# A hybrid decoder step on one core: operands of the second group made from x times g on ScalarE, without 1 / rms, and sums of weight blocks on VectorE

## The chip, the cores and the metric

The kernel runs on one core of a Trainium2 chip. A core has five engines with an instruction queue each, worked off in order: TensorE (PE: matmuls; PEld: its weight loads), VectorE (DVE), ScalarE (ACT), GpSimd (POOL) and SyncE (SP, which here issues the DMAs). Matmul results land in PSUM banks, everything else lies in SBUF. The metric is the device time of one execution in microseconds, as a median of runs.

## The reference, cut to what matters

One decoder layer for 1024 prompt tokens and 64 decode tokens, D = 1024, all in float32. After three mixers (a recurrence, a short convolution and an attention) whose outputs are `mixed`, it ends in

```python
x = x + mixed @ lw['w_out']
h2 = rmsnorm(x, lw['g_mlp'])
x = x + jnp.square(jax.nn.relu(h2 @ lw['w_up'])) @ lw['w_down']
gate = jax.nn.sigmoid(rmsnorm(x, lw['g_ple']) @ lw['w_ple_gate'])
x = x + gate * (p @ lw['w_ple_proj'])
# rmsnorm(x, g) = x * rsqrt(mean(x * x) + 1e-6) * g;  w_up is 1024 x 4096, w_down 4096 x 1024
```

1 / rms is one number for each token. It can be multiplied in ahead of the product with `w_up`, or after it and ahead of the square, since relu(r * a) = r * relu(a) for r > 0.

## The kernel before, in words

x is kept transposed: 8 blocks of 128 rows (features) by tokens. A float32 product is made from pieces: each operand is split into a high and a low part (`S.copy` to the high part on ScalarE, a subtraction for the low part on VectorE or GpSimd), and three matmuls are summed.

The tokens are cut in two groups, A (512) and B (576, "the second group"). Their MLPs run over 16 slices `fb` of 256 columns of w_up. For A, `up` (L1333) does 2 x 24 matmuls of 128x512, `down` (L1400) 8 x 6. A's 1 / rms is multiplied in after the matmuls, when the bank is read (L1341). For B, `up7` (L1348) makes each slice with 7 products of 12 matmuls of 128x288 in place of 8, from sums and differences of blocks of the weights and of x. The operands of the 7 products (x times gain times 1 / rms, in sums and differences, split in high and low) are made once, by `operands` (L1291), in two calls: ids 11, 2, 3, 4 into four buffers (tag "big" of pool `mpb`) that held B's mixed operands `mh`, `ml` until then, and ids 21, 1, 22 into pool `hpb`, which takes the room of A's operands `nh`, `nl`. Per k = 0 to 3 a call makes `hk` (features k and 4 + k; L1302), `tk` (differences; L1308 to L1314) and each operand's high part (L1316, ScalarE) and low part (L1317). `hk` and `tk` share four buffers, so that two k are in flight.

Per slice `up7` loads two raw pieces of w_up (tile `wr`, two buffers, 512 KB each), splits three blocks (`wh`, `wl`), makes four sums of blocks (`s0` to `s3`, L1354 to L1358, GpSimd before) and splits these (`wsh`, `wsl`, L1042 ScalarE and L1043 GpSimd). A piece's buffer is free for the next load when its casts, its subtractions and its sums are done. Products go to banks 0 to 3 in turn and are put together by VectorE (L1385: `c`, `u`, `v`), then relu and square (L1379), `ah` (L1380, ScalarE) and `al` (L1381, GpSimd). B's `down` writes banks 4 to 7 in turn and VectorE adds each to x (L1406); it is emitted a slice behind `up7`.

The order is the program's, moved by a scheduler at build time; each engine then works its own queue in order. Around the change it is: out_proj(B) (L1322: x of B += mixed @ w_out, two blocks of x for each slice of weights), last `up` of A, the last two `down` of A with B's `rms` and `operands` among them, then 16 rounds of `up7` and `down` of B, then the gate stage.

Of the kernel before, what the change touches and what calls it, by code (L numbers as in the profile page):

```python
# [24 lines left out]
AF = mybir.ActivationFunctionType  # L25
ALU = mybir.AluOpType
# [22 lines left out]
def hybrid_step(ctx: ExitStack, tc: tile.TileContext, I, O):  # L49
# [6 lines left out]
    def f(t):  # L56
        return t.bitcast(F32)
# [19 lines left out]
    acc = banks(0, 1, 2)  # L77
# [59 lines left out]
    def P1(name, i=0):  # L137
        return par[:, col[name] + i:col[name] + i + 1]
# [1065 lines left out]
    class Part:  # L1204
# [85 lines left out]
        def operands(self, gain, ids, pool, bufs):  # L1290


            n = self.n // 2
            out = {}
            for i in ids:
                t = pool.tile([128, 4, 2 * n], F32R, name=f"op{i}", tag="big", bufs=bufs)
                out[i] = t.rearrange("p k t -> p (k t)").rearrange("p (e k t) -> p e k t", e=2, k=4)
            need = set(ids)
            for k in range(4):
                h = self.act("hk", F32)  # L1300
                for e in range(2):
                    V.scalar_tensor_tensor(h[:, e], self.x[:, 4 * e + k], P1(gain, 4 * e + k), self.rb, op0=ALU.mult,  # L1302
                                           op1=ALU.mult)
                t = self.act("tk", F32)
                val = {11: h[:, 0, :n], 21: h[:, 1, :n], 22: h[:, 1, n:], 1: t[:, 0, :n], 2: t[:, 0, n:],
                       3: t[:, 1, :n], 4: t[:, 1, n:]}
                if need & {1, 2, 4}:
                    V.tensor_sub(val[1], h[:, 0, n:], val[11])  # L1308
                if need & {2, 4}:
                    V.tensor_sub(val[2], val[22], val[1])  # L1310
                if 4 in need:
                    V.tensor_sub(val[4], val[21], val[2])
                if 3 in need:
                    V.tensor_sub(val[3], val[22], h[:, 0, n:])  # L1314
                for i in ids:
                    S.copy(out[i][:, 0, k], val[i])  # L1316
                    (V if i in (21, 1, 22) else G).tensor_sub(out[i][:, 1, k], val[i], f(out[i][:, 0, k]))  # L1317
            return out

    w_up, w_down = I["w_up"][0], I["w_down"][0]  # L1320

    def out_proj(p, k0=0, nk=8, bank=acc):  # L1322
        nm = 16 // nk
        x = [h[k0 // 4:] for h in p.h]
        for m0 in range(0, 8, nm):
            w = load(w_out[k0 * 128:(k0 + nk) * 128, m0 * 128:(m0 + nm) * 128], nk, nm * 128)
            for m in range(m0, m0 + nm):
                for t0, n in p.chunks:
                    ps = bank()
                    gemm_p(ps, w, m - m0, x, t0, n, nk=nk)  # L1330
                    V.tensor_add(p.x[:, m, t0:t0 + n], ps[:, :n], p.x[:, m, t0:t0 + n])  # L1331
# [15 lines left out]
    def up7(p, fb, ops, pool):  # L1347
# [3 lines left out]
        a = {(m, k): r[k][:, :, 128 * m:128 * m + 128] for m in range(2) for k in range(2)}  # L1351
        s_ = [pool.tile([128, 512], F32, name=f"s{i}").rearrange("p (k c) -> p k c", k=4) for i in range(4)]
        w = {11: split_piece(a[0, 0])}
        G.tensor_add(s_[0], a[1, 0], a[1, 1])  # L1354
        G.tensor_sub(s_[1], s_[0], a[0, 0])
        G.tensor_sub(s_[2], a[0, 0], a[1, 0])
        w[12] = split_piece(a[0, 1])
        G.tensor_sub(s_[3], a[0, 1], s_[1])  # L1358
        w[22] = split_piece(a[1, 1])
        for i in (2, 1, 3, 4):  # L1360
            w[i] = split_piece(s_[i - 1], pool=pool, tag="ws", bufs=4)
# [14 lines left out]
        def out(m, e, c):  # L1376

            t = slice(e * n, e * n + n)
            V.scalar_tensor_tensor(c, c, 0.0, c, op0=ALU.max, op1=ALU.mult)  # L1379
            S.copy(ah[:, m, t], c)  # L1380
            G.tensor_sub(al[:, m, t], c, f(ah[:, m, t]))  # L1381

# [49 lines left out]
    for fb in range(1, NA):  # L1432
        u, before = up(A, fb), u
        down(*before)
    out_proj(B)
    B.rms(banks(6, 7))
    ops = B.operands("g_mlp", (11, 2, 3, 4), mpb, 4)
    for fb in range(NA, 16):
        u, before = up(A, fb), u
        if fb < 15:  # L1440
# [101 lines left out]
```

## Time and profile before

| | us |
|---|---|
| median of 3 runs (lowest, highest) | 1780.79 (1775.39, 1781.9) |
| profiled execution, its own time | 1778.32 |
| its span in the trace | 1776.6 |
| PE / DVE / ACT / POOL busy in the span | 1687.8 / 1097.3 / 743.7 / 746.1 |

How to read the rows below. A row of busy times names a stretch, its length, the busy us of each engine with the number of its instructions in brackets, the granted TensorE clock (1.00 is full), the busy share of the DMA engines and GB/s. A row of waits says which engine and line waited for which, with the total in us, how often and the longest. A row of a group names line, engine, operation, tile written <- tiles read, shapes, count, then busy us, mean ns of one, and the idle time ahead of them with its releaser. A row of a source answer gives durations as min/median/max in ns. A row of a timeline gives start and duration in us. Matmuls are pipelined: a busy PE is not a PE at full rate, and the pitch from start to start tells the rate. Buffer numbers are left out of names: `op` is any operand, `b` any bank, `s` any sum.

### The profile page before, as it was taken

Reading aid. Unit: us, or ns where it says so; the run is one execution under the profiler, and the core shown is the slowest. Engines: PE = TensorE matmul, PEld = TensorE weight load, DVE = VectorE, ACT = ScalarE, POOL = GpSimd, SP = SyncE. Lnnn points to the kernel's source line nnn. Section 1 sums busy time; section 2 is a strip of 40 time slices with the busy share of each in tenths; the row PEclk is TensorE's granted clock in tenths of the full one; section 3 lists DMA queues with packets and bytes.
Section 4 is the critical chain, followed back from the end, with each engine's and each line's share of the span. In section 5 each row is a group of like instructions: output and inputs, shape, how many; then the busy total and the mean of one; then the engine's idle time right before and its main releaser. Section 6 shows DMA issues by size and latency. Waiting matters only on the chain.

```text
span 1776.6 us, 30204 instructions
## 1 busy us (share of the span) xinstructions
PE 1687.8 (95%) x11741; PEld 1504.5 (85%) x11741; DVE 1097.3 (62%) x1788; ACT 743.7 (42%) x1459; POOL 746.1 (42%) x694
## 2 busy tenths in 40 slices
PE   6999899999999899999989999996989999999998
PEld 5898888888988778888866667985989999998898
DVE  6266954554676689887743434349867777677432
ACT  6634223323453567656533333433433333335421
POOL 4123322312301444323255532428887877764210
PEclk9999998999999899999999999998999999999999
DMA  5134356434524654433255544420333233232211
GB/s 182 50 118 134 107 150 174 117 90 118 138 81 132 190 165 123 123 122 93 85 149 167 168 132 130 134 72 24 95 95 96 88 92 96 84 93 63 74 51 39
DMA packets 206738, 196.98 MB, mean 111 GB/s; under 512 B 57794, under 2 KB 172130, under 8 KB 206467
## 3 DMA queue, kind: packets, MB, share of 16 engines
q1 hardware_dynamic: 201474, 178.27, 34.4%
q0 software_dynamic: 5120, 16.78, 3.2%
q8 instruction: 92, 1.51, 0.4%
q14 instruction: 52, 0.42, 0.1%
HBM read 158.02 MB, written 36.98 MB: 110 GB/s over the span
## 4 chain that ended last, share of the span: by engine, by line
PE 72%; DVE 12%; DMA 5%; issue 4%; ACT 3%; POOL 2%; SPq 2%; ACTq 0%; DVEq 0%; POOLq 0%
PE b L1062 12%; PE b L1064 12%; PE b L1063 12%; PE b L1369 3%; PE b L169 3%; PE b L1371 3%; PE b L1370 3%; PE b L170 3%; PE b L171 2%; PE b L790 2%; PE b L791 1%; PE b L792 1%; PE b L910 1%; DVE x L1406 1%; PE b L1192 1%
## 5 line engine op out<-in xcount | busy, mean ns | idle before, releaser
L1043 POOL TENSOR_TENSOR wl<-wr,wh 128x512 fp32r<-128x512 f32 x164 | 226.9, 1389 | 239.4 <-ACT wh L1042 220.0
L1042 ACT CAST wh<-wr 128x512 fp32r<-128x512 f32 x292 | 179.0, 623 | 342.7 <-PE b L1063 200.0
L1062 PE MATMUL b<-ah,wh 128*128 128x288 f32 (+1 forms) x768 | 257.2, 335 | 15.0 <-DVE x L1406 13.4
L1406 DVE TENSOR_TENSOR x<-b,x 128x288 f32<-128x288 f32 (+1 forms) x384 | 195.8, 528 | 95.4 <-PE b L1064 94.2
L1064 PE MATMUL b<-ah,wl 128*128 128x288 f32 (+1 forms) x768 | 252.7, 329 | 0.0
L1063 PE MATMUL b<-al,wh 128*128 128x288 f32 (+1 forms) x768 | 252.3, 329 | 0.0
L1062 PEld LDWEIGHTS b<-ah,wh 128*128 128x128 f32 x768 | 144.9, 189 | 33.4 <-DVE x L1406 17.8
L1062 PE MATMUL b<-nh,wh 128*128 128x512 f32 (+1 forms) x448 | 166.3, 372 | 2.5 <-DVE x L1331 1.6
L1063 PE MATMUL b<-nl,wh 128*128 128x512 f32 (+1 forms) x448 | 165.9, 370 | 0.0
L1064 PE MATMUL b<-nh,wl 128*128 128x512 f32 (+1 forms) x448 | 164.8, 368 | 0.0
L1064 PEld LDWEIGHTS b<-ah,wl 128*128 128x128 f32 x768 | 144.9, 189 | 10.3
L1063 PEld LDWEIGHTS b<-al,wh 128*128 128x128 f32 x768 | 145.3, 189 | 9.4 <-issue 0.8
L1043 DVE TENSOR_TENSOR wl<-wr,wh 128x512 fp32r<-128x512 f32 x128 | 110.7, 869 | 50.2 <-ACT wh L1042 46.2
L790 PE MATMUL b<-wh,h_hi 128*128 128x256 f32 x432 | 128.7, 298 | 2.0 <-ACT nat L797 2.0
L792 PE MATMUL b<-wh,h_lo 128*128 128x256 f32 x432 | 126.7, 293 | 0.0
L791 PE MATMUL b<-wl,h_hi 128*128 128x256 f32 x432 | 126.7, 293 | 0.0
L169 PE MATMUL b<-h_hi,wh 128*128 128x384 f32 (+1 forms) x336 | 115.9, 345 | 1.9 <-ACT xs L330 1.2
L890 DVE TENSOR_TENSOR_SCAN keep<-keep,onesq 128x128 f32<-128x128 f32 (+3 forms) x64 | 93.3, 1463 | 33.7 <-ACT keep L889 33.2
L170 PE MATMUL b<-h_lo,wh 128*128 128x384 f32 (+1 forms) x336 | 113.7, 338 | 0.0
L171 PE MATMUL b<-h_hi,wl 128*128 128x384 f32 (+1 forms) x336 | 112.9, 336 | 0.0
L159 POOL TENSOR_TENSOR wl<-wr,wh 128x1024 fp32r<-128x1024 f32 x26 | 68.8, 2656 | 94.1 <-ACT wh L158 94.1
L1062 PEld LDWEIGHTS b<-nh,wh 128*128 128x128 f32 x448 | 84.7, 189 | 18.8 <-DVE x L1406 2.6
(416 smaller groups left out, 4381.8 us busy)
## 6 DMA issues: line engine op xcount, KB each, us to landing
wr<-in_w_up SPq DMA_DIRECT2D x64, 512.0 KB
wr<-in_w_down SPq DMA_DIRECT2D x64, 512.0 KB
wr<-in_w_in SPq DMA_DIRECT2D x26, 512.0 KB
wr<-in_w_out SPq DMA_DIRECT2D x16, 512.0 KB
xt<-in_x_prompt SPq DMA_DIRECT2D x8, 512.0 KB
stk_s<-sth SPq DMA_DIRECT2D x32, 128.0 KB
stk_s<-stl SPq DMA_DIRECT2D x32, 128.0 KB
out<-nat SPq DMA_DIRECT2D x16, 256.0 KB
```

Of the source, the lines that this page charges most:

```text
L169: PE.matmul(ps[:, :n], wh[:, k, c], a, start=(k == 0), stop=False)
L170: PE.matmul(ps[:, :n], wh[:, k, c], b, start=False, stop=False)
L171: PE.matmul(ps[:, :n], wl[:, k, c], a, start=False, stop=(k == nk - 1))
L790: PE.matmul(o, a, w[0][:, k, :], start=(k == 0), stop=False)
L791: PE.matmul(o, a, w[1][:, k, :], start=False, stop=False)
L792: PE.matmul(o, b, w[0][:, k, :], start=False, stop=(k == 7))
L1042: S.copy(h3, src)
L1043: (sub or G).tensor_sub(l3, src, f(h3))
L1062: PE.matmul(ps[:, :n], w(0, k, m), a, start=(k == 0), stop=False)
L1063: PE.matmul(ps[:, :n], w(0, k, m), b, start=False, stop=False)
L1064: PE.matmul(ps[:, :n], w(1, k, m), a, start=False, stop=(k == nk - 1))
L1406: V.tensor_add(p.x[:, m, t0:t0 + n], ps[:, :n], p.x[:, m, t0:t0 + n])
```

## The change

Four edits:

- `operands` makes `hk` with ScalarE's copy with a scale (x times gain), 1 / rms left out. `out` of `up7` multiplies it in instead: relu(c) * rb on VectorE (where relu(c) * c stood), then a square on ScalarE as an instruction more.
- The low parts of the operands alternate between VectorE and GpSimd in place of a fixed share (VectorE for 21, 1 and 22, GpSimd for the others).
- The four sums of weight blocks of each `up7` move from GpSimd to VectorE.
- out_proj(B) works through its slices of w_out in the order 0, 4, 2, 6, so that blocks 0, 1, 4, 5 of x are final halfway, and the first call of `operands` stands ahead of `rms`.

```diff
             for k in range(4):
                 h = self.act("hk", F32)
                 for e in range(2):
-                    V.scalar_tensor_tensor(h[:, e], self.x[:, 4 * e + k], P1(gain, 4 * e + k), self.rb, op0=ALU.mult,
-                                           op1=ALU.mult)
+                    S.activation(h[:, e], self.x[:, 4 * e + k], AF.Copy, scale=P1(gain, 4 * e + k))
...
-                for i in ids:
+                for a, i in enumerate(ids):
                     S.copy(out[i][:, 0, k], val[i])
-                    (V if i in (21, 1, 22) else G).tensor_sub(out[i][:, 1, k], val[i], f(out[i][:, 0, k]))
+                    (V, G)[(a + k) % 2].tensor_sub(out[i][:, 1, k], val[i], f(out[i][:, 0, k]))
...
-    def out_proj(p, k0=0, nk=8, bank=acc):
+    def out_proj(p, k0=0, nk=8, bank=acc, order=None):
...
-        for m0 in range(0, 8, nm):
+        for m0 in order or range(0, 8, nm):
...
-        G.tensor_add(s_[0], a[1, 0], a[1, 1])
-        G.tensor_sub(s_[1], s_[0], a[0, 0])
-        G.tensor_sub(s_[2], a[0, 0], a[1, 0])
+        V.tensor_add(s_[0], a[1, 0], a[1, 1])
+        V.tensor_sub(s_[1], s_[0], a[0, 0])
+        V.tensor_sub(s_[2], a[0, 0], a[1, 0])
         w[12] = split_piece(a[0, 1])
-        G.tensor_sub(s_[3], a[0, 1], s_[1])
+        V.tensor_sub(s_[3], a[0, 1], s_[1])
...
-            V.scalar_tensor_tensor(c, c, 0.0, c, op0=ALU.max, op1=ALU.mult)
+            V.scalar_tensor_tensor(c, c, 0.0, p.rb[:, t], op0=ALU.max, op1=ALU.mult)
+            S.square(c, c)
...
-    out_proj(B)
+    out_proj(B, order=(0, 4, 2, 6))
+    ops = B.operands("g_mlp", (11, 2, 3, 4), mpb, 4)
     B.rms(banks(6, 7))
-    ops = B.operands("g_mlp", (11, 2, 3, 4), mpb, 4)
```

Three places show how the queues change, all in VectorE's. The first is where A's last down ends and the first round of `up7` begins; `x<-b` with 128x512 is the addition that frees a bank of A's down, L1302 makes `hk`, L1308 makes `tk`, op_12624 is operand 21, op_12625 operand 1, op_12626 operand 22. Before:

```order
L1406 TENSOR_TENSOR x<-b_12603,x 128x512
L1302 SCALAR_TENSOR_TENSOR hk<-x,par,rb 128x576 x2
L1406 TENSOR_TENSOR x<-b_12611,x 128x512
L1317 TENSOR_TENSOR op_12624<-hk,op_12624 128x288
L1317 TENSOR_TENSOR op_12625<-tk,op_12625 128x288
L1317 TENSOR_TENSOR op_12626<-hk,op_12626 128x288
```

After (the low parts are L1316 there, the sums L1353 to L1357):

```order
L1406 TENSOR_TENSOR x<-b_12603,x 128x512
L1406 TENSOR_TENSOR x<-b_12611,x 128x512
L1353 TENSOR_TENSOR s_12675<-wr 128x512
L1355 TENSOR_TENSOR s_12677<-wr 128x512
L1316 TENSOR_TENSOR op_12624<-hk,op_12624 128x288
L1316 TENSOR_TENSOR op_12626<-hk,op_12626 128x288
L1354 TENSOR_TENSOR s_12676<-s_12675,wr 128x512
L1316 TENSOR_TENSOR op_12625<-tk,op_12625 128x288
L1307 TENSOR_TENSOR tk<-hk 128x288
L1357 TENSOR_TENSOR s_12678<-wr,s_12676 128x512
```

The sixteen `hk` are gone from between the additions, and the `tk` of the first call have moved ahead of A's downs. The four sums, which stood in GpSimd's queue before, now come right behind A's last addition, between the low parts of the second call.

The second is a round of B in the steady state (`x<-b` with 128x288 frees a bank of B's down). Before:

```order
L1406 TENSOR_TENSOR x<-b_14939,x 128x288
L1406 TENSOR_TENSOR x<-b_14947,x 128x288
L1406 TENSOR_TENSOR x<-b_14955,x 128x288
L1385 TENSOR_TENSOR c<-b_15052,p_15037 128x288
L1379 SCALAR_TENSOR_TENSOR c<-c 128x288
L1406 TENSOR_TENSOR x<-b_14963,x 128x288
```

After:

```order
L1406 TENSOR_TENSOR x<-b_14939,x 128x288
L1406 TENSOR_TENSOR x<-b_14947,x 128x288
L1353 TENSOR_TENSOR s_15344<-wr 128x512
L1406 TENSOR_TENSOR x<-b_14955,x 128x288
L1354 TENSOR_TENSOR s_15345<-s_15344,wr 128x512
L1357 TENSOR_TENSOR s_15347<-wr,s_15345 128x512
L1406 TENSOR_TENSOR x<-b_14963,x 128x288
```

Three of the four sums now stand among the additions that free down's banks; the first of them, s0, reads both raw pieces of w_up.

The third is later in a round, where the last products are put together. Before:

```order
L1385 TENSOR_TENSOR c<-b_15120,v 128x288
L1379 SCALAR_TENSOR_TENSOR c<-c 128x288
L1385 TENSOR_TENSOR c<-b_15138,u_15113 128x288
L1379 SCALAR_TENSOR_TENSOR c<-c 128x288
L1043 TENSOR_TENSOR wl<-wr,wh 128x512
L1406 TENSOR_TENSOR x<-b_15176,x 128x288
```

After:

```order
L1385 TENSOR_TENSOR c<-b_15154,v 128x288
L1355 TENSOR_TENSOR s_15659<-wr 128x512
L1378 SCALAR_TENSOR_TENSOR c<-c,rb 128x288
L1385 TENSOR_TENSOR c<-b_15173,u_15146 128x288
L1378 SCALAR_TENSOR_TENSOR c<-c,rb 128x288
L1043 TENSOR_TENSOR wl<-wr,wh 128x512
L1406 TENSOR_TENSOR x<-b_15212,x 128x288
```

The fourth sum, s2, comes in ahead of a relu, and so ahead of the next four additions.

## Rows read from the trace of the kernel before

**Rows 1.** Busy time of each engine in stretches of the span

```profile
1190.00:1260.00 70.00, 50.23 (x261) 42.44 (x260) 66.62 (x84) 24.39 (x55) 51.99 (x42) 0.90 0.12 35
1260.00:1350.00 90.00, 84.38 (x615) 83.06 (x614) 64.91 (x113) 32.80 (x64) 78.00 (x62) 0.98 0.33 98
1350.00:1575.00 225.00, 225.00 (x1693) 225.00 (x1692) 158.16 (x289) 77.18 (x148) 180.31 (x141) 1.00 0.30 90
```

**Rows 2.** Busy time in stretches of 10 us, for the granted clock

```profile
1230.00:1240.00 10.00, 4.84 (x23) 4.32 (x21) 10.00 (x9) 4.47 (x10) 8.38 (x6) 0.67 0.01 2
...
1320.00:1330.00 10.00, 9.56 (x59) 9.42 (x60) 6.43 (x15) 2.96 (x6) 6.48 (x6) 0.83 0.23 71
```

**Rows 3.** PE's matmuls by form, 1190 to 1260 (first of three alike)

```profile
L1062 PE MATMUL b<-ah,wh 128*128 128x512 f32 x31 | 12.8, 412 | 4.8 <-DVE x L1406 4.8
```

**Rows 4.** Timeline of PE in A's down: two starts, 17 matmuls apart

```profile
1193.16 0.40 PE L1062 MATMUL b<-ah,wh 128*128 128x512 f32 x1
...
1197.03 0.39 PE L1064 MATMUL b<-ah,wl 128*128 128x512 f32 x1
```

**Rows 5.** What PE waited for, 1150 to 1360

```profile
PE b L1370 <- DVE op L1317: 11.0, 4, 5.2
PE b L1062 <- DVE x L1406: 10.3, 7, 2.7
PE b L1369 <- DVE x L1406: 2.1, 1, 2.1
```

**Rows 6.** VectorE's instructions by form, 1190 to 1260

```profile
L1302 DVE SCALAR_TENSOR_TENSOR hk<-x,par,rb 128x576 f32<-128x576 f32 x16 | 17.7, 1142 | 0.2 <-ACT rb L1282 0.2
L1406 DVE TENSOR_TENSOR x<-b,x 128x512 f32<-128x512 f32 x16 | 10.8, 679 | 0.7 <-PE b L1064 0.7
L1317 DVE TENSOR_TENSOR op<-hk,op 128x288 fp32r<-128x288 f32 x8 | 8.1, 1043 | 0.0
L1308 DVE TENSOR_TENSOR tk<-hk 128x288 f32<-128x288 f32 x8 | 6.8, 852 | 0.0
```

**Rows 7.** VectorE's lines of products and weights: durations, the whole span

```profile
L1379 DVE SCALAR_TENSOR_TENSOR c<-c x64: 449/1066/1617, 1247.5 to 1606.0; 128x288 f32<-128x288 f32 x64
L1385 DVE TENSOR_TENSOR c<-b,u x32: 442/458/460, 1247.1 to 1605.5; 128x288 f32<-128x288 f32 x32
L1043 DVE TENSOR_TENSOR wl<-wr,wh x37: 674/691/1786, 1360.1 to 1574.9; 128x512 fp32r<-128x512 f32 x37
```

**Rows 8.** ScalarE's instructions by form, 1190 to 1260 and 1177 to 1190

```profile
L1316 ACT CAST op<-hk 128x288 fp32r<-128x288 f32 x12 | 4.9, 430 | 9.6 <-DVE hk L1302 9.6
L1042 ACT CAST wsh<-s 128x512 fp32r<-128x512 f32 x8 | 4.5, 614 | 0.0
...
L1260 ACT ACTIVATE sq<-x 128x576 f32<-128x576 f32 x1 | 0.7, 685 | 0.1
```

**Rows 9.** GpSimd's sums and subtractions by form, 1350 to 1575

```profile
L1043 POOL TENSOR_TENSOR wsl<-s,wsh 128x512 fp32r<-128x512 f32 x36 | 53.3, 1503 | 0.5
...
L1354 POOL TENSOR_TENSOR s<-wr 128x512 f32<-128x512 f32 x10 | 13.0, 1296 | 21.6 <-DMA wr<-in_w_up 21.6
```

**Rows 10.** What the DMA queue waited for before it issued, 1350 to 1575

```profile
SPq L1036 <- POOL s L1355: 72.7, 10, 8.1
```

**Rows 11.** Timelines of VectorE in a round of B, and of GpSimd and PE there

```profile
1421.84 0.46 DVE L1406 TENSOR_TENSOR x<-b,x 128x288 f32<-128x288 f32 x1 [0.34 <-PE b L1064]
...
1422.99 1.29 POOL L1354 TENSOR_TENSOR s<-wr 128x512 f32<-128x512 f32 x1 [1.92 <-DMA wr<-in_w_up]
...
1423.43 0.46 DVE L1406 TENSOR_TENSOR x<-b,x 128x288 f32<-128x288 f32 x1 [1.14 <-PE b L1064]
...
1435.67 1.48 DVE L1379 SCALAR_TENSOR_TENSOR c<-c 128x288 f32<-128x288 f32 x1
...
1441.36 1.54 DVE L1406 TENSOR_TENSOR x<-b,x 128x288 f32<-128x288 f32 x4
...
1442.40 0.30 PE L1062 MATMUL b<-ah,wh 128*128 128x288 f32 x1
```

## The prediction

> **What bounds the kernel now.** The page comes first: PE is busy for 95% of the span, so the question is where PE does not run at its pitch. The table of busy times by stage answers it. From 1350 to 1575 us, the steady rounds of B, PE has 1693 matmuls in 225.00 us and never waits: 0.1329 us each [rows 1], so that a round of 84 + 96 matmuls takes 23.9 us. That is the rate of a bound PE, and nothing that frees another engine can gain there. The two stretches ahead of it are not at that rate.
>
> 1190 to 1260 us is the hand-over from A to B. Of its 261 matmuls 94 have 512 columns (three lines of 31, 31 and 32 [rows 3]), at a pitch of (1197.03 - 1193.16) / 17 = 0.228 us [rows 4]; 157 have 288 columns; ten small ones take 1.0 us together (an estimate; the rows below do not hang on it). At full pitch that is 94 x 0.228 + 157 x 0.1329 + 1.0 = 43.3 us of 70. **26.7 us are lost.** 1260 to 1350 us has 615 matmuls, 81.7 us of work in 90: **8.3 us lost** [rows 1].
>
> Why, is in what PE waited for: low parts of operands from VectorE (11.0 us) and VectorE's additions that free banks (10.3 and 2.1 us) [rows 5]. VectorE was busy for 66.6 of the 70 us [rows 1]. Of that the `hk` took 17.7, the additions of A's down 10.8, low parts and `tk` most of the rest [rows 6]. What is not a wait is the clock: after the waits it was granted at 0.67 from 1230 to 1240 [rows 2], which is in the 26.7. So the hand-over is bound by VectorE's queue.
>
> **The change part by part.**
>
> *`hk` to ScalarE.* It takes 17.7 us out of VectorE's 66.6 and adds 16 ScalarE instructions of about 0.69 us (a square of the same 128x576 tile takes 685 ns [rows 8]): 11 us on an engine that was busy for 24.4 of the 70 us [rows 1]. Without 1 / rms, half of the first call's `hk` and `tk` move ahead of 1177 us, into out_proj(B). No more than half: `hk` and `tk` have four buffers, and the operands themselves are written into the buffers of `mh` and `ml`, which out_proj(B) reads to its end. The order 0, 4, 2, 6 is what makes these two k possible, and costs nothing by itself, as the loads and matmuls are the same in number.
>
> *What is late next in the hand-over.* A's last two downs run with nothing between VectorE's additions, 0.68 us each [rows 6] against six matmuls of 0.228 = 1.37 us in PE: the waits for additions end. ScalarE has to deliver the high part of A's last `up` before the last down; in its queue that stands behind casts, `hk` and six of the squares of `rms`, and I count it there only 1 to 2 us early. I take 2 us lost (0 to 8). Then PE has operand 11 (12 matmuls, 1.6 us) and two k of operand 21 (0.8 us) to run, 2.4 us. The next matmuls want the cast of s1, which ScalarE does behind the copy of the first product (1.6 us, then 0.4) and four `hk` (4 x 0.69): 1.6 + 0.4 + 2.8 + 0.61 [rows 8] = 5.4 us, so PE waits 3.0. VectorE has s1 earlier, since GpSimd's queue is empty there. Behind that come the last k of the low parts and the four splits of the sums on GpSimd (1.29 to 1.5 us each [rows 9]), and banks that wait for VectorE behind the next round's sums: 4 us by the same count. So 7 us (3 if only the first wait shows, 12 if VectorE's instructions take their contended time). For the clock after a wait I take 2 us (0 to 3): 1320 to 1330, at 0.83 after one wait, had 59 matmuls where 75 fit [rows 2], 2.1 us. The hand-over keeps 2 + 7 + 2 = 11 of 26.7 and **gives back 15.7** (3.7 to 23.7).
>
> *Sums to VectorE, 1260 to 1350.* Here GpSimd was busy for 78 of 90 us [rows 1], and a raw buffer was freed by its sums: in the rounds after, the DMA queue waited 72.7 us for s1 alone [rows 10]. Four sums of 1.30 us [rows 9] leave GpSimd in each round of about 24 us, and on VectorE one takes from 0.69 us (the same shape as `wl` [rows 7]). Weights of down land earlier; I leave 2 us (0 to 6), so **6.3 come back** (2.3 to 8.3).
>
> *Sums on VectorE, every round.* In the steady rounds nothing can be gained, and VectorE goes from 158.2 / 225 = 70% busy [rows 1] to 70% + 4 x 0.69 / 24 = 82% or, at the longest time in the row of `wl`, 1.79 us [rows 7], to 100%. Two places matter. s0 waits for the second raw piece, which in the round shown landed when GpSimd's s0 started, 1422.99; VectorE comes to it after its third addition of that quarter, about 1421.5. The fourth, which started at 1421.84, slips to about 1423.7 and the next one by 2 us [rows 11]; with four banks PE comes back to a bank three groups of 0.80 us after it left it, so this is just hidden. s2 lies tighter: four additions from 1441.36 on free the banks of down, at 0.385 us each, the first by 1441.75, and PE wants that bank at 1442.40 [rows 11]: 0.65 us to spare. s2 takes 0.69 us if alone (0.04 lost) and about 1.3 if it stands behind a GpSimd instruction (0.65 lost). GpSimd's own s2 has left that place, so part of the time comes back. I take 0.25 us a round, 14 rounds: **3.5 us** (0 to 9).
>
> *The factor moved behind the matmuls* costs VectorE nothing: relu(c) * rb has the shape of relu(c) * c. ScalarE gets 64 squares of 128x288, 0.43 us each going by the cast of that shape [rows 8], four a round: 1.7 us on an engine busy for 77.2 / 225 = 34%. The square lengthens the way from `c` to `al`, but down of that slice runs a round later. Free, unless that lag is lost; then 0.43 us a round, 6 us.
>
> *Low parts in turns* moves 2 us from one engine to the other and is inside the counts above.
>
> On contention the rows speak against moving sums to VectorE. Its relu, which reads SBUF alone, takes 449 ns at best and 1066 in the median, while the addition of a bank to an SBUF tile of the same shape takes 442 to 460 [rows 7]: something holds up what reads SBUF twice. The Trainium skill (SBUF — State Buffer, Who interferes with whom) states that a VectorE instruction with two SBUF inputs contends with a GpSimd instruction that reads SBUF, and that the one that comes second waits for the whole of the other. The trace agrees as far as these two rows go. By the rule alone each of four sums a round would wait out a GpSimd instruction.
>
> **The sum.** 15.7 + 6.3 - 3.5 = 18.5 us. Against the profiled execution's 1778.3 that is 1759.8; the median of the runs is 2.5 above that execution, so **1762**.
>
> **Rivals.**
>
> *ScalarE becomes the limit of the hand-over.* Its queue gets the 16 `hk` ahead of the high part of A's last `up`, and I count that part only 1 to 2 us early. For it: the queue is in order, and each wait for a buffer of `hk` pushes all that follows. Against: it is busy for a third of the time. If it is 8 us late in place of 2, and the products wait 10 in place of 7, 9 us of the gain go: 1771. Chance 0.17.
>
> *Contention takes more.* By the mechanism of the relu row, every s2 stands behind a GpSimd instruction: 0.65 x 14 = 9 us in place of 3.5, so 1767.5; this is what the rule on SBUF would do here. Chance 0.15.
>
> *VectorE bounds the rounds: slower.* If the second raw piece lands late against VectorE's queue, s0 holds additions and PE stands in all 14 rounds. The place is the quarter with 1421.84; the price is what s0's wait exceeds the hidden 2 us by. The hand-over and the stretch after it give 22.0, so from 1.6 us a round it decides; at 2.5 us a round it is 35 - 22 = 13 us slower: 1794. For it: the landing follows VectorE's own `wl`, so a late VectorE makes it later still. Against: s1 and s3 on VectorE free the raw buffers sooner, and the average load is 82%. Chance 0.10.
>
> *More comes back.* With contention gone on both sides the hand-over keeps only 5 us and the rounds cost nothing: 21.7 + 8.3 = 30, 1751. Chance 0.13.
>
> That the operands don't get ahead at all (the order of x's blocks useless, since their buffers are held) is not a rival with a sign of its own: `hk` still leaves VectorE's queue.
>
> **How the numbers follow.** The forecast (1762, by its own bounds 1754 to 1772) has 0.45. The range takes in the two dearer cases and the cheaper one and leaves out most of the slower one: 1750 to 1780. What a measurement of this kernel can tell from no change is about 0.5%, 9 us: faster is below 1772, slower above 1790. Faster: 0.45 x 0.95 + 0.17 x 0.5 + 0.15 x 0.8 + 0.13 = 0.76; slower 0.08, as the slower case begins at its deciding point; the same 0.16.
>
> **What would show it.** In the profile after, 1190 to 1260 should have VectorE well below 66 of 70 us and PE near 60 busy, with few waits of PE for operands and no clock under 0.8; the next 90 us should have over 650 matmuls. In the rounds PE's pitch should stay at 0.133; a pitch over 0.14 with PE waiting for VectorE's additions would show the slower case. I am wrong in the first step if PE in the hand-over waits for ScalarE's `ah` or for casts of sums by more than 10 us.

## The result, and the profile after

After: 1767.19 us (median of 6 runs, 1761.68 to 1769.77); before, on the same chip, 1781.35 (6 runs, 1775.39 to 1787.41). The ratio is **0.9916, 95% interval 0.9889 to 0.9942**: 15 us faster (10 to 20), where 1762 and 18.5 us had been forecast. The profiled execution took 1763.72 us (span 1762.0) against 1778.32.

Not all of that difference of 14.6 us is the change. I set marks on program points in the timelines of PE and ScalarE: the last matmul of out_proj(B); the copy of `p` (L1389), once per round of `up7`, the first and the sixth of them; and the last matmul of B's last down. The outer two in PE's timeline of the kernel after (columns as in [rows 11]):

```profile
1174.73 0.29 PE L1064 MATMUL b<-mh,wl 128*128 128x288 f32 x1
...
1633.71 0.29 PE L1064 MATMUL b<-ah,wl 128*128 128x288 f32 x1
```

That is 458.98 us; the kernel before has 1177.12 and 1648.34 there, 471.22. So **the change is worth 12.2 us** in this pair of profiles. What lies behind the last mark is 128.3 us in both, and 2.4 us lie ahead of the first. Executions scatter more than that there: a kernel below (e4), whose queues are those of the kernel after up to that point, reached it at 1170.55. So these 2.4 us can't be credited to the change.

The windows that answer [rows 1], with the one ahead of them (busy us of PE, PEld, DVE, ACT, POOL with their counts, granted clock, DMA share, GB/s):

```profile
1177.00:1190.00 13.00, 11.65 (x52) 9.32 (x50) 13.00 (x16) 11.22 (x24) 9.60 (x9) 1.00 0.23 63
1190.00:1260.00 70.00, 57.63 (x331) 51.18 (x332) 58.98 (x81) 36.94 (x77) 46.24 (x36) 0.95 0.21 64
1260.00:1350.00 90.00, 88.23 (x655) 87.07 (x655) 70.92 (x132) 36.03 (x71) 50.13 (x41) 1.00 0.32 98
1350.00:1575.00 225.00, 224.38 (x1679) 223.21 (x1678) 178.60 (x328) 94.96 (x189) 121.71 (x104) 1.00 0.29 86
```

VectorE fell from 66.6 to 59.0 us in the hand-over and GpSimd from 78 to 50 in the stretch behind it; VectorE rose from 158 to 179 in the steady rounds, GpSimd fell from 180 to 122. By the forecast's own count, 1190 to 1260 now has 84 matmuls of 512 columns, 227 of 288 and 20 small ones: 19.1 + 30.2 + 2.0 = 51.3 of 70, so **18.7 us are lost in place of 26.7**. The next 90 us lose 90 - 655 x 0.1329 = 3.0 in place of 8.3. New is a loss of 1.1 us ahead of 1190 (52 matmuls of 512 columns in 13 us), where VectorE is busy for all of the 13 us.

What PE waited for from 1170 to 1300, which answers [rows 5] (us in total, times, longest):

```profile
PE b L1062 <- DVE x L1406: 5.6, 9, 1.7
PE b L1368 <- DVE c L1385: 2.4, 1, 2.4
PE b L1062 <- DVE r L1340: 2.4, 1, 2.4
PE b L1368 <- DVE u L1385: 2.2, 1, 2.2
PE b L1368 <- ACT wsh L1042: 2.0, 1, 2.0
PE b L1369 <- DVE op L1316: 0.9, 2, 0.6
```

The 11.0 us for low parts have shrunk to 0.9. But the engine that is late is still VectorE, in five rows of six. One of its stops, in the second round of B (VectorE's timeline):

```profile
1247.85 0.69 DVE L1353 TENSOR_TENSOR s<-wr 128x512 f32<-128x512 f32 x1 [1.57 <-DMA wr<-in_w_up]
1248.58 1.82 DVE L1354 TENSOR_TENSOR s<-s,wr 128x512 f32<-128x512 f32 x1
1250.31 0.44 DVE L1385 TENSOR_TENSOR u<-b,u 128x288 f32<-128x288 f32 x1
1250.68 1.38 DVE L1357 TENSOR_TENSOR s<-wr,s 128x512 f32<-128x512 f32 x1
1251.99 0.44 DVE L1385 TENSOR_TENSOR c<-b,u 128x288 f32<-128x288 f32 x1
```

The sum s0 holds the queue for its load, s1 and s3 take 1.82 and 1.38 us beside GpSimd in place of 0.69, and the `c` for which PE waits 2.4 us stands behind them.

### The profile page after: what moved, and what is told of

Its sections match the earlier page's. It is cut to its first block, busy times and chain, and to the rows that moved or that the text cites. A ratio compares the mean times of both kernels' runs of the same rounds, so it can differ in the third digit from the quotient of the medians.

```text
span 1762.0 us, 30342 instructions
## 1 busy us (share of the span) xinstructions
PE 1683.0 (96%) x11741; PEld 1500.2 (85%) x11741; DVE 1115.4 (63%) x1838; ACT 779.8 (44%) x1539; POOL 649.7 (37%) x628
## 4 chain that ended last, share of the span: by engine, by line
PE 68%; DVE 14%; DMA 6%; issue 4%; ACT 3%; SPq 2%; POOL 2%; ACTq 0%; DVEq 0%; POOLq 0%
PE b L1062 12%; PE b L1064 11%; PE b L1063 11%; DMA wr<-in_w_up 3%; PE b L1368 2%; PE b L1370 2%; PE b L1369 2%; PE b L169 2%; PE b L170 2%; PE b L171 2%; DVE x L1406 2%; PE b L790 2%; DVE wl L1043 2%; PE b L791 1%; PE b L792 1%
## 5 line engine op out<-in xcount | busy, mean ns | idle before, releaser
L1406 DVE TENSOR_TENSOR x<-b,x 128x288 f32<-128x288 f32 (+1 forms) x384 | 191.7, 527 | 68.8 <-PE b L1064 66.2
```

## The experiments

All in one table: us from out_proj(B)'s last matmul to the first copy of p, from there to the sixth, from there to B's last down, the sum, and the ratio to the kernel before, with its 95% interval. In the rows with a star the scheduler gave PE another order of the rounds, and more of the work stands ahead of the sixth copy of p: 788 matmuls of 288 columns behind the first mark in e2, 774 in f1 and 789 in e4, where the kernel after has 749 and the one before 747. At 0.1329 us each their second part is too long, and their third too short, by 5.2, 3.3 and 5.3 us. The sum does not suffer.

| kernel | to p 1 | p 1 to p 6 | p 6 to down | sum | ratio (interval) |
|---|---|---|---|---|---|
| before | 45.5 | 124.3 | 301.4 | 471.2 | 1 |
| after | 42.3 | 115.6 | 301.1 | 459.0 | 0.9916 (0.9889, 0.9942) |
| e1: sums alone | 44.4 | 125.3 | 309.3 | 479.0 | 1.0046 (1.0025, 1.0067) |
| e2: all but the sums* | 42.7 | 121.4 | 306.1 | 470.2 | 0.9988 (0.9967, 1.0009) |
| g1: sums and square | 44.4 | 122.0 | 300.9 | 467.3 | 0.9977 (0.9959, 0.9996) |
| f1: e2, third raw buffer* | 42.6 | 118.9 | 296.3 | 457.8 | 0.9925 (0.9897, 0.9953) |
| f2: e1, third raw buffer | 46.3 | 124.1 | 318.6 | 489.1 | 1.0135 (1.0102, 1.0167) |
| f3: after, third raw buffer | 43.8 | 114.7 | 300.1 | 458.5 | 0.9944 (0.9923, 0.9965) |
| e4: sums of two rounds back* | 42.7 | 127.3 | 308.5 | 478.6 | 1.0006 (0.9985, 1.0027) |
| e3: old order of out_proj | 42.3 | 115.8 | 300.9 | 458.9 | 0.9919 (0.9887, 0.9950) |
| e5: low parts on VectorE | 42.8 | 117.1 | 303.1 | 462.9 | 0.9940 (0.9919, 0.9960) |
| e6: low parts on GpSimd | 39.0 | 116.5 | 301.2 | 456.6 | 0.9901 (0.9875, 0.9927) |
| g2: first p on VectorE | 43.8 | 117.1 | 299.9 | 460.8 | 0.9940 (0.9919, 0.9960) |
| h1: low parts mixed | 39.0 | 114.5 | 301.0 | 454.5 | 0.9905 (0.9881, 0.9929) |

### The change in two halves: e1 and e2

e1 is the kernel before with this alone, e2 the kernel after with this taken back:

```diff
-        G.tensor_add(s_[0], a[1, 0], a[1, 1])
+        V.tensor_add(s_[0], a[1, 0], a[1, 1])
```

(and so for the other three sums.)

> The kernel before with one edit: the four sums of weight blocks on VectorE. Theory (the hand-over is bound by VectorE's queue, the stretch after it by GpSimd's): 1190 to 1260 us loses 3 to 8 us more, because eight sums of 0.7 to 1.5 us join a queue that was busy 66.6 of 70 us; 1260 to 1350 loses about 3 in place of 8.3; the steady rounds stay at a pitch of 0.133; the time is within 4 us of the kernel before. Rival one (GpSimd's load is what slows VectorE's instructions in the hand-over too, so the sums are the part that pays): 8 us or more faster. Rival two (VectorE becomes the bound of the rounds): pitch over 0.137 from 1350 to 1575, 6 us or more slower.

> The kernel after with the sums back on GpSimd; all else stays. Theory (two gains in two places): the hand-over keeps its gain or more, since eight sums leave VectorE there (13 to 18 us lost in 1180 to 1260 against 20 in the kernel after), but 1260 to 1350 loses about 8 again in place of 3; the time is 2 us better to 5 us worse than the kernel after, ratio to before 0.991 to 0.995. Rival one (nearly all of the gain is that of the sums): ratio 0.998 or more. Rival two (the sums cost more than they bring): ratio 0.988 or less.

e1 was slower by 0.46%, 7.8 us between the marks; e2 gained 1.0 us, within its interval nothing. Added up, that is +6.8 us; together they gain 12.2. **The two halves work only together.** Where, the windows show, first of e1, then of e2:

```profile
1190.00:1260.00 70.00, 54.11 (x284) 47.01 (x282) 69.16 (x96) 26.25 (x57) 47.54 (x38) 0.88 0.17 53
1260.00:1350.00 90.00, 84.40 (x603) 82.03 (x603) 74.23 (x124) 30.97 (x59) 51.67 (x42) 0.98 0.30 88
1350.00:1575.00 225.00, 220.14 (x1632) 217.12 (x1631) 177.76 (x321) 77.99 (x144) 127.76 (x100) 1.00 0.29 87
```

```profile
1190.00:1260.00 70.00, 58.51 (x315) 51.50 (x314) 48.72 (x68) 33.90 (x70) 52.02 (x42) 0.90 0.18 53
1260.00:1350.00 90.00, 86.12 (x644) 85.42 (x644) 61.48 (x112) 37.27 (x76) 77.97 (x62) 1.00 0.32 97
1350.00:1575.00 225.00, 218.83 (x1613) 214.62 (x1613) 153.47 (x278) 88.59 (x180) 168.54 (x135) 1.00 0.28 84
```

The same count of lost time as above (from 1190 to 1260 e1 has 79 matmuls of 512 columns and 205 of 288, e2 99, 196 and 20 small ones):

| us lost by PE | 1177 to 1190 | 1190 to 1260 | 1260 to 1350 | 1350 to 1575 |
|---|---|---|---|---|
| before | 0 | 26.7 | 8.3 | 0 |
| e1: sums alone | 0 | 24.7 | 9.9 | 8.1 |
| e2: all but the sums | 0 | 19.4 | 4.4 | 10.6 |
| after | 1.1 | 18.7 | 3.0 | 1.9 |

Ahead of 1350 us the sums alone give back 0.4 us, the other half 11.2 and both 12.2, so there the sums bring next to nothing, with the other half or without it. The windows catch the four kernels at somewhat different work, so here are the same matmuls: from the 250th to the 750th of 288 columns behind the first mark before, e1, e2 and after lose 8.2, 6.1, 4.7 and 3.1 us. Of the 5.1 us gained in that stretch the sums bring 1.6 to 2.1, and ahead of it they cost 0.5 to 1.7. In the steady rounds each half costs 8 to 11 us by itself, and both together 2. That is where the sums pay: with them, and with the order of the rounds that came with them, the loss that the other half brings by itself is gone.

1632 and 1613 matmuls stand in the steady window where before had 1693. For e1 the theory missed both stretches; rival two's signs came out (225 / 1632 = 0.138 us each, 8 us slower), but not by load, as VectorE is busy for 178 of 225 us there, as in the kernel after: each round loses 0.5 us or more. For e2 rival one came nearest by its ratio, for a reason it did not name; the theory was right that the hand-over keeps its gain, and wrong on 1260 to 1350 and on the rounds. Both rounds had to be looked into.

### Why the sums alone cost 0.5 us a round: g1

In e1 each round has this (timelines of VectorE, GpSimd, the DMA queue, ScalarE and PE, put together):

```profile
1488.88 2.20 POOL L1381 TENSOR_TENSOR al<-c,ah 128x288 fp32r<-128x288 f32 x2 [0.86 <-ACT ah L1380]
...
1489.11 1.30 DVE L1043 TENSOR_TENSOR wl<-wr,wh 128x512 fp32r<-128x512 f32 x1
...
1491.72 0.39 ACT L1389 COPY p<-b 128x288 f32<-128x288 f32 x1
...
1491.80 0.68 DVE L1043 TENSOR_TENSOR wl<-wr,wh 128x512 fp32r<-128x512 f32 x1
...
1492.50 0.37 SPq L1036 DMA_DIRECT2D wr<-in_w_up  x1
...
1496.32 0.69 DVE L1354 TENSOR_TENSOR s<-wr 128x512 f32<-128x512 f32 x1 [2.20 <-DMA wr<-in_w_up]
...
1497.30 1.61 DVE L1355 TENSOR_TENSOR s<-s,wr 128x512 f32<-128x512 f32 x1
...
1499.02 0.69 DVE L1358 TENSOR_TENSOR s<-wr,s 128x512 f32<-128x512 f32 x1
...
1499.63 1.54 DVE L1406 TENSOR_TENSOR x<-b,x 128x288 f32<-128x288 f32 x4
...
1500.13 0.40 PE L1062 MATMUL b<-ah,wh 128*128 128x288 f32 x1 [0.40 <-DVE x L1406]
```

Read it downwards. `wl` stands beside GpSimd's `al` and takes 1.30 us; four additions stand between it and the next `wl`, which frees a raw buffer; so the load of the next raw piece is issued 0.78 us after the copy of p; s0 waits for it until 4.60 us after that copy; s1 takes 1.61 us beside GpSimd; the additions start behind s3, and PE waits. The same place in the kernel after:

```profile
1475.09 0.68 DVE L1043 TENSOR_TENSOR wl<-wr,wh 128x512 fp32r<-128x512 f32 x1
...
1475.40 1.82 POOL L1381 TENSOR_TENSOR al<-c,ah 128x288 fp32r<-128x288 f32 x2 [1.40 <-ACT ah L1380]
...
1477.70 0.39 ACT L1389 COPY p<-b 128x288 f32<-128x288 f32 x1
...
1477.86 0.37 SPq L1036 DMA_DIRECT2D wr<-in_w_up  x1
```

There the square on ScalarE makes `ah`, and so `al`, come later: `wl` starts first and takes 0.68, the additions and the second `wl` come earlier, and the load is issued 0.16 us after the copy of p. If that is the cause, the square alone must cure e1. g1 adds it, with the two SBUF inputs of the relu kept:

```diff
-            V.scalar_tensor_tensor(c, c, 0.0, c, op0=ALU.max, op1=ALU.mult)
+            V.scalar_tensor_tensor(c, c, 0.0, c, op0=ALU.max, op1=ALU.max)
+            S.square(c, c)
```

> The kernel before with the sums on VectorE and the square on ScalarE: VectorE makes relu(c) from c and c, two SBUF inputs as before, ScalarE the square. Operands keep 1 / rms. Theory (with the sums alone, al on GpSimd stood beside the wl that frees down's raw buffer: 1.30 us in place of 0.68, so the next raw piece was issued 0.79 us after the copy of p in place of 0.16, s0 started 4.5 us after it in place of 4.0, and each round was longer by what s0 is later than 4.0; the square sends al out of wl's way): wl 0.7 us there, s0 at most 4.1 us after the copy of p, rounds of 23.9 to 24.1 us, 301 to 303 us from the sixth copy of p to B's last down in place of 309; the hand-over stays at 168 to 171 us; ratio to before 0.999 to 1.001. Rival (it is not the square, but what else the kernel after changes): rounds stay at 24.4 us or more, ratio 1.004 or more.

It does: 300.9 us from p 6 on in place of 309.3. The same rows in g1's timelines: `wl` ahead of `al` and short, s0 3.98 us after the copy of p:

```profile
1488.69 0.68 DVE L1043 TENSOR_TENSOR wl<-wr,wh 128x512 fp32r<-128x512 f32 x1
...
1488.98 1.81 POOL L1382 TENSOR_TENSOR al<-c,ah 128x288 fp32r<-128x288 f32 x2 [1.40 <-ACT ah L1381]
...
1491.29 0.39 ACT L1390 COPY p<-b 128x288 f32<-128x288 f32 x1
...
1495.27 0.69 DVE L1354 TENSOR_TENSOR s<-wr 128x512 f32<-128x512 f32 x1 [1.57 <-DMA wr<-in_w_up]
```

Up to p 6 it took 166.4 us, 3.4 less than before and less than expected, which puts its ratio below both expectations; I did not look for the reason.

The timelines allow more. In the eight kernels whose rounds have this order on VectorE (after, e1, e3, e5, e6, g1, g2, h1) I took each round from about 1350 us on but the last: the time from the copy of p to s0, and to the next copy of p. In 66 of 67 rounds the length is 23.94 us, and longer by what s0 starts later than 3.98 us after the copy, to 0.05 us. Three rounds of after: 3.89 gives 23.93, 4.27 gives 24.25, 5.03 gives 25.02; of e1: 4.47 gives 24.46, 5.81 gives 25.79. (One round of g1 lost 0.46 elsewhere.) The round with 5.03, copy of p, s0 and next copy:

```profile
1404.65 0.39 ACT L1389 COPY p<-b 128x288 f32<-128x288 f32 x1
...
1409.68 0.69 DVE L1353 TENSOR_TENSOR s<-wr 128x512 f32<-128x512 f32 x1 [2.63 <-DMA wr<-in_w_up]
...
1429.67 0.39 ACT L1389 COPY p<-b 128x288 f32<-128x288 f32 x1
```

The kernel after sits at the edge: s0 at 3.79 to 4.27 in all other rounds. That a landing is later now and then stays unexplained.

### Why all but the sums cost 0.5 us a round: f1

In e2 most rounds took 25.0 to 25.3 us. VectorE's timeline of one, with a cast of ScalarE ahead of it:

```profile
1478.13 1.14 ACT L1042 CAST wh<-wr 128x512 fp32r<-128x512 f32 x2 [7.02 <-DMA wr<-in_w_down]
...
1478.79 0.69 DVE L1043 TENSOR_TENSOR wl<-wr,wh 128x512 fp32r<-128x512 f32 x1 [3.23 <-ACT wh L1042]
...
1480.37 0.45 DVE L1385 TENSOR_TENSOR u<-b,p 128x288 f32<-128x288 f32 x1
...
1482.34 1.62 DVE L1378 SCALAR_TENSOR_TENSOR c<-c,rb 128x288 f32<-128x288 f32 x1
...
1484.35 1.07 DVE L1378 SCALAR_TENSOR_TENSOR c<-c,rb 128x288 f32<-128x288 f32 x1
...
1485.83 1.07 DVE L1378 SCALAR_TENSOR_TENSOR c<-c,rb 128x288 f32<-128x288 f32 x1
1486.82 0.45 DVE L1406 TENSOR_TENSOR x<-b,x 128x288 f32<-128x288 f32 x1
```

The raw piece of down lands late, `wl` stands at the head of VectorE's queue for 3.2 us, `u` comes late, and three relus beside GpSimd stand ahead of the addition that PE wants. Is it the raw buffers or the relus? f1, f2 and f3 are e2, e1 and after with a third raw buffer; room for it comes from one buffer less for split weights:

```diff
-        raw = wpool.tile([128, 1024], F32, name="wr", bufs=2)
+        raw = wpool.tile([128, 1024], F32, name="wr", bufs=3)
...
-    def split_piece(src, sub=None, pool=None, tag="w", bufs=10):
+    def split_piece(src, sub=None, pool=None, tag="w", bufs=9):
```

> The kernel after with the sums on GpSimd, and a third raw buffer (wr 3 in place of 2; paid for with 9 in place of 10 buffers of split weights). Without the third buffer this kernel's rounds took 25.05 us in place of 23.94, and from the sixth copy of p to B's last down 306.1 us in place of 301.1. Theory (the raw buffers' loop: a buffer is freed by the sums, its load lands late, the cast waits for it by up to 8 us, VectorE stands behind the cast at wl and reaches the relus and the additions late): rounds of 23.9 to 24.1 us, 301 to 303 us for that part, waits of casts for weights down from 70 us to under 25 in 1350 to 1600. Rival (relus of 1.05 us beside a GpSimd that never rests: occupancy and contention): rounds stay at 24.8 to 25.1 us, 305 us or more.

> The kernel before with the sums on VectorE, and a third raw buffer (9 buffers of split weights in place of 10). Without it the rounds took 24.5 us and from the sixth copy of p to B's last down 309.3 us. Theory (s0 on VectorE waits 2.1 to 3.4 us for the second raw piece, over the 1.8 us that the additions can bear): with a third buffer the piece is loaded a buffer earlier, s0 waits under 1 us, rounds of 23.9 to 24.1 us, 301 to 303 us. Rival (VectorE's own occupancy, 79% with sums of 1.6 us beside GpSimd): rounds stay at 24.4 to 24.6 us, 307 us or more. The hand-over is as without the third buffer in both.

> The kernel after with a third raw buffer (9 buffers of split weights in place of 10). Theory of the raw buffers' loop: the wait of VectorE for s0 (1.4 to 2.6 us a round) goes, the two rounds of 25.0 us become 23.9, and of the hand-over's 157.9 us (from out_proj(B)'s end to the sixth copy of p) the stop at 1252 us, 4 us behind a wait for a raw piece, goes: 3 to 6 us faster than the kernel after, ratio to before 0.988 to 0.990. Rival (what is left is VectorE's own instructions; the loads are hidden): within 1 us of the kernel after, ratio 0.991 to 0.992; a buffer less of split weights may cost 1 to 3 us.

f1: the raw buffers. Its rounds take 23.9 us, its sum is 457.8, 12.4 us better than e2 and as good as the kernel after **with all sums on GpSimd**. The largest of ScalarE's waits from 1350 to 1600, in e2, then the largest in f1:

```profile
ACT wh L1042 <- DMA wr<-in_w_down: 50.7, 7, 8.0
```

```profile
ACT wh L1042 <- PE b L1063: 101.6, 40, 3.8
```

No cast of f1 waits for a load there; they wait for their buffers of split weights, which PE's matmuls set free. The stretch ahead of the rounds gains too, with GpSimd as busy as in e2: it loses 90 - 671 x 0.1329 = 0.8 us in place of 4.4.

```profile
1260.00:1350.00 90.00, 89.40 (x671) 88.94 (x670) 65.58 (x120) 38.92 (x81) 77.38 (x62) 1.00 0.32 101
```

So raw buffers are what e2 lacks. Why two were enough before and are not in e2 is open: the square came in, but the scheduler also gave the rounds another order, and e4 below, in nearly e2's order on PE but with the sums on VectorE, has rounds as long. The two were not tried apart.

f2 went against both of its expectations: rounds of 25.6 us. The scheduler, with another buffer, puts s0, a `wl` and s1 (1.78 us) in a row ahead of additions, and PE waits 1.3 to 1.5 us once a round; g1, not f2, settles e1. f3 has the same row, with s1 at 0.69 us, and its rounds are 23.92 to 24.01 from about 1360 us on. s0 still waits for its load there (1.75 us), but starts 1.9 us after the copy of p in place of 4.0, and PE waits no longer for it. Its first rounds did not gain, though, and its ratio is worse than either expectation: it reached the first mark 4.7 us later than the kernel after did, by scatter or by the missing buffer of split weights. That was not tried apart.

### The first rounds: e4, e3, g2

e4 puts the sums of two rounds back, e3 undoes the order of out_proj(B), g2 takes the first copy of p from ScalarE:

```diff
-        V.tensor_add(s_[0], a[1, 0], a[1, 1])
+        (G if fb < 2 else V).tensor_add(s_[0], a[1, 0], a[1, 1])
...
-    out_proj(B, order=(0, 4, 2, 6))
+    out_proj(B)
...
-        S.copy(p1, product(11, 11))
+        (V.tensor_copy if fb == 0 else S.copy)(p1, product(11, 11))
```

> The kernel after with the sums of the first two rounds on GpSimd, those of rounds 2 to 15 on VectorE. Theory one (the sums pay in the stretch after the hand-over, because GpSimd's queue there is what frees the raw buffers, from the first round on): from out_proj(B)'s end to the sixth copy of p 161 to 164 us in place of 157.9, rounds as in the kernel after, ratio 0.993 to 0.996. Theory two (in the hand-over VectorE is the late one, with sums of 1.3 to 1.8 us among its low parts, and the sums pay only from the third round on): 153 to 157 us, ratio 0.988 to 0.991.

> The kernel after with out_proj(B) in its old order 0, 2, 4, 6. Theory (the order lets hk and tk of two k go ahead of 1177 us, and without it they fall into the hand-over, where VectorE is full): six tk and the low parts behind them, some 6 x 0.7 to 1.2 = 4 to 7 us of VectorE, come later; PE loses 3 to 6 us more in 1177 to 1260, ratio 0.993 to 0.996. Rival (the operands' buffers are held by out_proj(B) to its end, so what is early is only waiting): within 1 us of the kernel after, ratio 0.991 to 0.992.

> The kernel after with the first round's copy of p on VectorE in place of ScalarE. Theory one (ScalarE stood 7.3 us at that copy, the bank not yet done, with four hk, the casts of sums and of operands behind it): hk start 2 to 4 us earlier, the waits of PE at the first products (0.6, 2.0 and 2.3 us) shrink, from out_proj(B)'s end to the sixth copy of p 153 to 156 us in place of 157.9, ratio 0.988 to 0.991. Theory two (the hk could not have started, since their buffers are freed by low parts that VectorE makes behind A's last addition, 1217.2 us): within 1 us of the kernel after, 157 to 159 us, ratio 0.991 to 0.993.

e4: neither. With the shift of its sixth copy counted, it lost 7 us in the first rounds and 13 in the later ones, though those have the sums on VectorE. The scheduler had set their order anew, as in e2: s0 now stands 0.6 us ahead of the copy of p, and waits for its load 2.2 to 2.9 us in the steady rounds, which take 24.5 to 26.2 us. So e4 says nothing of where the sums pay; it says that 24 us rounds hang on an order that an edit in other rounds can change.

e3: within 0.1 us of the kernel after. The order of out_proj(B) brings nothing.

g2: the `hk` did start 8 us earlier, at 1209.32 in place of 1217.32, and the time to p 6 became 3 us longer, not 2 to 4 shorter. The waits at the first products changed places and summed to 5.1 us as in the kernel after, and between 1240 and 1300 PE waited 8.7 us for VectorE in place of 6.0, the longest time 3.6 for an addition. ScalarE is not what bounds the hand-over.

### Whose are the low parts: e5, e6, h1

```diff
-                    (V, G)[(a + k) % 2].tensor_sub(out[i][:, 1, k], val[i], f(out[i][:, 0, k]))
+                    V.tensor_sub(out[i][:, 1, k], val[i], f(out[i][:, 0, k]))
```

for e5; in e6 it is `G`, in h1 `G` in the first call and in turns in the second.

> The kernel after with all low parts of the operands on VectorE, none on GpSimd (14 instructions of 128x288 more for VectorE). Theory (in the hand-over VectorE's instructions that read SBUF alone take 1.06 to 1.8 us because GpSimd streams beside them, 0.45 to 0.69 when it doesn't): with GpSimd empty of low parts each of VectorE's takes about 0.5, so the 14 more cost 7 and the rest gives 7 to 12 back; PE loses 15 to 21 us in 1180 to 1260 against 20, ratio 0.989 to 0.993. Rival (it is the number of instructions that counts): 14 x 1.1 = 15 us more on a full queue, PE loses 28 to 35 us there, ratio 0.996 to 1.0.

> The kernel after with all low parts of the operands on GpSimd (14 fewer on VectorE). Theory one (in 1177 to 1200 us VectorE is full and PE waits 6.4 us for its additions and relus of A): these waits fall under 2 us, GpSimd gets 14 x 0.8 to 1.0 = 12 us more and has room (46 of 70 us); 153 to 156 us from out_proj(B)'s end to the sixth copy of p in place of 157.9, ratio 0.987 to 0.991. Theory two (GpSimd's low parts stand ahead of the splits of the sums, and slow VectorE beside them): what is won before 1200 is lost at the first products, 157 to 161 us, ratio 0.991 to 0.995. The rounds from the sixth on stay at 23.9 to 24.1 us in both.

> The kernel after with the low parts of the first call of operands all on GpSimd, those of the second call in turns as in the kernel after. With both calls on GpSimd, out_proj(B)'s end to the first copy of p took 39.0 us in place of 42.3, but PE then waited for GpSimd's low parts of the second call and for VectorE behind them. Theory: 39 us to the first copy of p is kept, and from there to the sixth copy 112 to 116 us in place of 116.5, 151 to 155.5 us in all in place of 157.9; ratio to before 0.986 to 0.990, better than both kernels. Rival (in the second call VectorE and GpSimd only change places, and each low part on VectorE delays a sum and an addition): 118 us or more from the first copy to the sixth, 157 to 160 in all, ratio 0.991 to 0.993. The rounds from the sixth copy on stay at 23.9 to 24.1 us but for a landing that is late now and then.

e5 from 1177 to 1190:

```profile
1177.00:1190.00 13.00, 13.00 (x61) 10.83 (x60) 12.21 (x28) 13.00 (x30) 2.64 (x2) 1.00 0.28 82
```

VectorE does 28 instructions in 12.2 us where the kernel after does 16 in 13.0. The instructions are not the same, so take one form: a low part made from `tk` takes 0.45 us in the mean (9 of them) beside a GpSimd that is busy for 2.6 us, and 1.06 (3 of them) beside one that is busy for 9.6. So half of the theory holds, the price of contention. The other half fell: the next low parts met GpSimd's `wl` and sums of `rms` (1.69 and 1.55 us each), and an addition that PE waited 3.2 us for stood behind them. It is 4 us worse than the kernel after, 2 of them up to p 6 and 2 in the rounds, where s0 was late more often (up to 5.40 us after the copy of p); its ratio lies between the two expectations.

e6 confirms theory one: in the hand-over's first part VectorE was the late engine. From out_proj(B)'s end to the first copy of p it takes 39.0 us in place of 42.3; PE's waits for VectorE up to 1215 us are 1.0 us there:

```profile
PE b L1062 <- DVE x L1406: 1.0, 2, 0.6
```

where the kernel after has 2.4 and 2.0. h1 keeps that and takes 114.5 from there to p 6: 153.5 us in all, within the theory's 151 to 155.5, 4.5 us better than the kernel after between the marks. Its ratio is just above the theory's 0.986 to 0.990. Its median is 1760.03 (before beside it 1780.46). By the traces h1 is the best of all; by the ratios, 0.9905 against 0.9916, the runs do not tell it from the kernel after.

## Why the prediction was right, point by point

**What bounds the kernel: right.** PE in the rounds, VectorE's queue in the hand-over, raw buffers in the stretch behind it (f1). The time was right as well (1767 in a range of 1750 to 1780), but by the width of the range more than by its terms: the two gains came to 12.2 us where 22.0 had been forecast.

**`hk` to ScalarE: 15.7 us forecast, 6.9 measured** (18.7 + 1.1 us lost in place of 26.7; inside the range of 3.7 to 23.7; e2, without the sums, gives 7.3). The step that was mis-sized is what the hand-over keeps, 11 us forecast and 19.8 measured, in two of its terms. *A's downs*: 2 us forecast, for ScalarE's late `ah`; 4.9 measured (the stops that end at 1191.0, 1194.4 and 1197.8), and for VectorE. Half of the operands' work that moved ahead of 1177 piled up between 1177 and 1190, because the operands' buffers are held by out_proj(B) to its end (so the kernel has it; no run frees them sooner), and there 16 instructions took 13.0 us. I had counted what leaves the hand-over and not what fills the place it goes to. e6 and h1 show it: without those low parts 3.3 us come back. *First round's products*: 3.0 + 4 forecast; the first wait is 2.9 (0.8 and 2.1), but what follows in the first two rounds costs 7.5, since the next rounds' sums stand in VectorE's queue at 1.3 to 1.8 us each; the forecast had that time as its upper bound only. The rest, 4.5, is the clock (0.83 granted from 1220 to 1240) and small matmuls, where 2 stood.

**Sums, 1260 to 1350: 6.3 forecast, 1.4 to 2.1 measured**, below the range of 2.3 to 8.3. The stretch as a whole gave 5.3 back, but 3.9 of them come without the sums (e2: 4.4 lost in place of 8.3), and the sums alone give none there (e1: 9.9 lost), or 2.1 between the same matmuls. The step that failed took GpSimd's load for what holds the raw buffers: GpSimd is busy for 78.0 of these 90 us before, for as long in e2, and for 77.4 in f1, which loses 0.8. [rows 10] could not show it: it comes from the steady rounds, where PE lost nothing, and in the same answer a wait of the DMA queue for VectorE stands ahead of it:

```profile
SPq L1036 <- DVE wl L1043: 73.5, 8, 9.8
```

**Sums in the rounds: 0.25 us a round forecast, 0.2 measured** (the nine rounds from the sixth copy of p on took 217.4 us, nine of the kernel before at 23.95 would take 215.6); what follows them gave 1.8 back. The size was right and the place wrong. I had priced s2 among the additions (0.65 us to spare), where nothing was lost, and called the wait of s0 "just hidden". It is s0 that decides, by a relation of one to one. What the sums bring to the other half, 11.2 us between the marks (e2 against the kernel after), comes to 10 us in the rounds, where the forecast had them as a loss alone.

**The factor behind the matmuls, squares on ScalarE: "free" is wrong.** With the sums on GpSimd that half loses about 10 us in the rounds (e2: 306.1 + 5.2 us in place of 301.4), by way of the raw buffers (f1), though the square is not told apart from the new order there; with the sums on VectorE the square brings 8.4 us (g1 against e1), since it sends `al` out of the way of `wl`.

**Order of out_proj(B), low parts in turns.** The first costs nothing, as said, and brings nothing (e3). The second was put at about nothing; it costs 4.5 us against the best share (h1).

**The rivals.** *VectorE bounds the rounds* is a real mechanism: e1 is that case, with the place (s0 ahead of the additions) and the price per us that the rival named. The kernel after sits at its edge. *Contention takes more*: the price was right (1.30 for 0.68), the place another. The Trainium skill (SBUF — State Buffer, Who interferes with whom) has it that a VectorE instruction with two SBUF inputs and a GpSimd instruction that reads SBUF contend, and that the order of issue decides which of them blocks. The trace agrees: where `wl` starts ahead of `al` it takes 0.68 us, where it starts behind it 1.30. *ScalarE limits the hand-over*: no (g2).

## What to carry to other kernels

Two halves of a change can each be worth nothing or less and be worth 12 us together: here each spoiled the steady rounds by a path of its own, and the other took that path away. So try the halves apart before adding their terms up. Before comparing two kernels between marks, count the work between the marks: a mark in one engine's queue can stand elsewhere in another's. A queue that waits in a stretch where the bounding engine loses nothing says little about what bounds another stretch. Where a round is just hidden, find the one instruction that waits for a transfer ahead of work that another engine wants, and measure its start against a fixed point of the round; the length of the round then follows to a twentieth of a us. And work moved ahead of a busy stretch lands in another stretch: count what is there.

## What I had not expected of the hardware

- A VectorE subtraction of 128x512 with two SBUF inputs took 0.68 us when it started 0.3 us ahead of a GpSimd subtraction, and 1.30 when it started 0.2 us behind it. A square of 0.45 us on ScalarE, which made that subtraction come later, was thus worth 0.5 us a round on PE.
- From 1177 to 1190 VectorE's low parts made from `tk`, 128x288, took 1.06 us in the mean with GpSimd busy for 9.6 of the 13 us (after), and 0.45 with GpSimd busy for 2.6 (e5).
- Equal queues came to the same matmul at 1174.73 and at 1170.55 us in two executions (after and e4): 4 us that no edit accounts for, as much as several of the effects above. Marks in the program tell such edits apart where spans do not.
